# A fused encoder layer on one core: the steps of the state-space unit handed out one for each block of k's and q's projections, where k's blocks took two

## The chip, the cores and the metric

One Trainium2 chip, of which the kernel uses one core. The metric is the device time of the whole kernel in microseconds (us); the median of several runs is quoted. TensorE (PE) does the matmuls, VectorE (DVE) and GpSimd (POOL) elementwise work, ScalarE (ACT) activation functions and scaled copies; SyncE (SP) issues most DMAs.

## The reference

The layer takes `x` of 1024 tokens by 1024 columns in float32. The first half of it, in which the change lies, is `x <- x + W_out . groupRMS(concat[gMLP, S5, attention](W_in . RMSNorm(x)))`; a mixture of 16 experts follows. The three mixers share one input projection `W_in`. Cut to what matters here:

```python
def s5_mixer(u, ...):                      # u: 1024 tokens x 256 channels, 16 groups of 16 channels
    bu = einsum('gph,blgh->blgp', b_bar, ug)             # 64 complex states a group
    _, states = lax.associative_scan(combine, (a, bu), axis=1)
    y = einsum('ghp,blgp->blgh', c_mat, states).real
    y = gelu(y + d * u)
    return y * sigmoid(y @ glu_w + glu_b)

def band_attention(q, k, v, q_g, k_g, rel_bias):   # 8 heads of 64
    q, k = rms_norm(q, q_g), rms_norm(k, k_g)
    ...                                    # each chunk of 64 tokens sees itself and the 8 chunks before it
```

## The kernel before, in words

The normalised input stands transposed in SBUF as 8 pieces of 128 columns, each as a high and a low part (`hTh`, `hTl`), and every weight is split in the same way when it arrives: `load_w` fetches four pieces of 256 rows by 512 columns (`rw`), ACT copies the high part (`wh`, line 126) and DVE subtracts (`wl`, line 127). A product is then three matmuls (lines 130 to 132: high by high, low weight, low input).

A *block* is the projection of 128 tokens on 512 columns: 8 input pieces by 3 matmuls, 24 matmuls into one of two PSUM banks (`pj`, tag `acc`). The kernel does 8 blocks of k, then 8 of q, then 8 of v. For k and q each block is followed by a scaled copy (`kt` or `qt`, line 617), a square (`sqk`, line 619) and a sum over each head (`s`, line 620); every second block adds a reciprocal root on DVE (nine small instructions, lines 109 to 118: `rq_h`, `rq_y`, `rq_a`, `r`) and a product (line 624). v's blocks (`vt`, line 877) are interleaved with the transposition of k and q per head (`k_T`, `q_T`: lines 651 to 681) and with the first two sets of attention scores (lines 711 to 723), for which the Exp function's table is loaded on ACT at line 864.

The state-space unit S5 is a Python generator, `s5()`, that gives up control 21 times; `tick(n)` runs its next n steps. The steps in order:

- 1 to 3: transposed input (`u5`), powers and rotations for the first groups, `taps(0)`.
- 4 to 15: four rounds b = 0 to 3 of four groups each, three steps a round. The first step is `scan(b)` and `outputs(b)`: PE makes `s5v` (line 517, 16 matmuls), DVE multiplies by the rotation, adds, and scans (`zz`, lines 519, 520 and 522), POOL and DVE rotate back (`f`, line 527), and the output taps `w2` are made (lines 534 to 538; the trace calls the tile `w`). The second is `rotation(b+1)` (`cs`, `cst`: lines 504 and 505 on DVE, 506 to 509 on POOL). The third is `taps(b+1)` (`s5a` on PE, lines 483 and 484, whose copies are ACT's), `result(b)` (`s5y` on PE, lines 546 and 547; Gelu on ACT, line 549) and `powers(b+2)` (lines 473 to 475).
- 16 to 19: two halves of the gate: transpositions (`yTp` on PE, line 577; `yT` on ACT, line 579), then `glu` on PE (line 584), a sum on DVE (line 586), Sigmoid on ACT (line 587), a product on POOL (line 589).
- 20 and 21: a norm of each half of `y5`: square on ACT (line 598), sum on DVE (line 601), root, product on POOL.

After v's blocks `tick(100)` runs whatever steps are left, and attention follows. Tiles of the second PSUM tag, `big`, have three buffers, which S5's `s5a`, `s5v`, `s5y`, `yTp` and `glu` share with the transpositions of k and q and with the scores. Weights live in a ring of SBUF buffers; the pieces 0 and 1 of q's weights (written r0, r1 below; r2 and r3 are the others) are in a second ring.

In which order the instructions of these loops stand on an engine is made by the scheduler of the language from the program's order, free buffers and its own estimate of readiness; each engine then works strictly through its own queue. Attention's order is written out by hand and begins behind v's last block.

Of the kernel before, what the change touches and what calls it, by code (L numbers as in the profile page):

```python
# [31 lines left out]
def trunk(tc, A, dbg=None, upto="all"):  # L32
# [35 lines left out]
    def slot(name, shape, dt=F32, far=None):  # L68
        far = name in FAR if far is None else far
        return slots.tile(shape, dt, name=name, tag="far" if far else "slot", bufs=FARS if far else SLOTS)  # L70
# [7 lines left out]
    def acc(name, shape, dt=F32):  # L78
        return psum.tile(shape, dt, name=name, tag="acc", bufs=2)

    def bc(ap, shape):
        return ap.to_broadcast(shape)
# [7 lines left out]
    def tick(n=1):  # L90

        while n and side:
            try:
                next(side[0])
                n -= 1
            except StopIteration:
                side.pop(0)
# [23 lines left out]
    def rsqrt(*args):  # L121
        for _ in rsqrt_steps(*args):
            pass
# [58 lines left out]
    def proj(out, sel, w, ks=range(KD)):  # L182
        his, los = w
        for k in ks:
            mm3(out, hT[k][:, sel], lT[k][:, sel], his[k], los[k], k == ks[0], k == ks[-1])
# [108 lines left out]
    def tmp(shape, p=128):  # L294
        n = 1
        for q in shape[1:]:
            n *= q
        o = carve["o"]
        carve["o"] = o + n
        assert o + n <= 1024  # L300
        v = carve["t"][0:p, o:o + n]
        if len(shape) == 3:
            v = v.rearrange("p (a b) -> p a b", a=shape[1])
        if len(shape) == 4:
            v = v.rearrange("p (a b c) -> p a b c", a=shape[1], b=shape[2])
        return v
# [102 lines left out]
    kt = tmp([128, NG, 16])  # L409
# [198 lines left out]
    def qk_proj(name, w):  # L608
        out = []
        for tb in range(NT):  # L610
            a = acc("pj", [128, 512])
            proj(a, slice(tb * 128, (tb + 1) * 128), w)
            if tb % 2 == 0:
                out.append(slot(name, [128, 2, 512]))
                s16 = small.tile([128, 2, 8], F32, name="s16")
                r16 = small.tile([128, 2, 8], F32, name="r16")
            act.activation(out[-1][:, tb % 2], a, AF.Copy, scale=rs[:, tb:tb + 1])
            sq = work.tile([128, 512], F32, name="sqk", tag="w2")
            act.activation(sq, a, AF.Square, scale=rs[:, tb:tb + 1])
            dve.tensor_reduce(s16[:, tb % 2], sq.rearrange("p (h c) -> p h c", c=64), axis=AX.X, op=OP.add)  # L620
            if tb % 2 == 1:
                rsqrt(r16.rearrange("p a b -> p (a b)"), s16.rearrange("p a b -> p (a b)"), 16, 1.0 / 64)
                ov = out[-1].rearrange("p t (h c) -> p t h c", c=64)
                dve.tensor_tensor(ov, ov, bc(r16[:, :, :, None], [128, 2, 8, 64]), op=OP.mult)
            tick(2 if name == "kt" else 1)
        return out

    kt_ = qk_proj("kt", W["k"])
    W["q"] = load_w(768, 512, (0, 1))
    qt_ = qk_proj("qt", W["q"])  # L630
    W["v"] = load_w(1792, 512, (3,))
    gqk = const("gqk", [128, 2])
# [1021 lines left out]
```

## Time and profile before

| | us |
|---|---|
| median of 3 runs | 834.27 |
| lowest, highest run | 831.81, 837.59 |
| the profiled execution | 835.0 |
| its span in the trace | 833.1 |

The profiled execution is the one whose rows are read below, so a sum over rows is made against 835.0 us. The span is cut into busy time, waits and the granted clock of TensorE: a stretch's clock of 1.00 is 2.4 GHz, and 0.50 would be 1.2 GHz. "Waits" lists the idle time of an engine by what ended it. In the profiled execution k's blocks run from about 93.5 us to 171 us, q's from 183 us to 234 us and v's to 282.5 us; between k's and q's blocks lies a stretch of 12 us with S5's last round and half of its gate.

### The profile page before, as it was taken

The numbers are of one execution on the slowest core, as the hardware profiler recorded it, in microseconds if no ns is written. First come the engines' busy times: TensorE is split into PE (matmuls) and PEld (weight loads), VectorE is DVE, ScalarE is ACT, GpSimd is POOL, SyncE is SP. The second block draws the span as 40 slices with busy tenths as digits, with TensorE's granted clock in tenths as the row PEclk, the third lists the DMA queues.
The fourth block names the chain that finished last, engine by engine and source line by source line (L and its number), as shares of the span: only waits on it lengthen the run. The fifth ranks groups of instructions, "written<-read, shape, count | busy, mean of one in ns | idle before, by whom it ended". The sixth has DMA issues, their size and how long they took to land. (4 is left out here: it accounts for less than half of the span.)

```text
span 833.1 us, 13661 instructions
## 1 busy us (share of the span) xinstructions
PE 755.7 (91%) x5024; PEld 640.0 (77%) x5025; DVE 530.1 (64%) x1266; ACT 400.9 (48%) x751; POOL 200.4 (24%) x235
## 2 busy tenths in 40 slices
PE   5999998989999887888888999968899999999995
PEld 4878777868888777888887888747678778888884
DVE  5866799873651467787877544677675774575541
ACT  6763432223343467777774323434454654464441
POOL 0000245411410332212101121112242433243221
PEclk9999999999999989999999999998999999999998
DMA  8423011330000400001045323286889999899663
GB/s 312 138 57 102 6 15 15 54 114 0 2 1 1 126 26 2 1 27 52 2 132 188 140 101 127 76 306 201 286 283 279 328 349 315 223 308 309 130 154 54
DMA packets 56516, 111.31 MB, mean 134 GB/s; under 512 B 24272, under 2 KB 28880, under 8 KB 56432
## 3 DMA queue, kind: packets, MB, share of 16 engines
q1 hardware_dynamic: 46880, 84.14, 30.0%
q0 software_dynamic: 6480, 23.60, 11.9%
q10 hardware_dynamic: 3072, 2.49, 1.0%
q8 instruction: 47, 0.77, 0.4%
q14 instruction: 37, 0.30, 0.1%
HBM read 90.05 MB, written 20.17 MB: 132 GB/s over the span
## 5 line engine op out<-in xcount | busy, mean ns | idle before, releaser
L130 PE MATMUL pj<-wh,hTh 128*128 128x512 f32 x256 | 104.2, 408 | 0.4 <-ACT hTh L209 0.3
L131 PE MATMUL pj<-wl,hTh 128*128 128x512 f32 x256 | 101.6, 397 | 0.0
L132 PE MATMUL pj<-wh,hTl 128*128 128x512 f32 x256 | 100.5, 398 | 0.1
L130 PE MATMUL gup<-gh,hgh 128*128 128x256 f32 x304 | 89.8, 295 | 1.7 <-ACT hgh L1278 0.2
L132 PE MATMUL gup<-gh,hgl 128*128 128x256 f32 x304 | 86.8, 286 | 3.1 <-DVE hgl L1282 3.1
L131 PE MATMUL gup<-gl,hgh 128*128 128x256 f32 x304 | 86.0, 283 | 0.0
L1325 PE MATMUL yp<-rwd,hh 128*128 128x256 f32 (+1 forms) x264 | 84.4, 457 | 0.0
L977 DVE TENSOR_TENSOR gl<-rwg,gh 128x1024 fp32r<-128x1024 f32 x64 | 78.0, 1241 | 7.3 <-ACT gh L972 6.5
L972 ACT ACTIVATE gh<-rwg 128x1024 fp32r<-128x1024 f32 x64 | 64.1, 1052 | 1.4 <-ACTq L1581 0.4
L1325 PEld LDWEIGHTS yp<-rwd,hh 128*128 128x128 f32 x264 | 45.8, 190 | 23.2 <-issue 17.4
L130 PEld LDWEIGHTS gup<-gh,hgh 128*128 128x128 f32 x304 | 57.9, 191 | 6.1 <-ACT y L1334 5.2
L132 PEld LDWEIGHTS gup<-gh,hgl 128*128 128x128 f32 x304 | 58.2, 191 | 4.5 <-DVE hgl L1282 3.6
L131 PEld LDWEIGHTS gup<-gl,hgh 128*128 128x128 f32 x304 | 58.2, 191 | 0.1
L132 PEld LDWEIGHTS pj<-wh,hTl 128*128 128x128 f32 x256 | 48.1, 188 | 12.7 <-DVE hTl L210 1.3
L130 PEld LDWEIGHTS pj<-wh,hTh 128*128 128x128 f32 x256 | 48.5, 190 | 12.0 <-ACT hTh L209 1.3
L1337 POOL DMA_INDIRECT out<-y,ix x22 | 38.2, 1735 | 78.9 <-ACT y L1334 45.9
L127 DVE TENSOR_TENSOR ptl<-ps,pth 128x640 fp32r<-128x640 f32 (+2 forms) x53 | 39.7, 749 | 26.5 <-ACT pth L126 26.1
L131 PEld LDWEIGHTS pj<-wl,hTh 128*128 128x128 f32 x256 | 48.4, 189 | 10.4
L130 PE MATMUL po<-pth,v_h 128*64 128x128 f32 x236 | 47.8, 232 | 2.9 <-DVE oc L765 2.0
L1334 ACT ACTIVATE y<-yp 128x512 f32<-128x512 f32 (+1 forms) x44 | 21.6, 491 | 59.6 <-PE yp L1325 59.6
L1262 POOL DMA_INDIRECT hg<-h2d,ix x22 | 23.8, 1080 | 105.2 <-PE yp L1325 69.5
L732 PE MATMUL ps<-ident,st 128*128 128x128 f32 x240 | 38.5, 290 | 9.8 <-ACT st L723 9.2
(390 smaller groups left out, 1974.9 us busy)
## 6 DMA issues: line engine op xcount, KB each, us to landing
rwg<-in_w_gu SPq DMA_DIRECT2D x62, 512.0 KB, 9.0
rwd<-in_w_down SPq DMA_DIRECT2D x32, 512.0 KB, 6.6
rw<-in_w_in SPq DMA_DIRECT2D x18, 512.0 KB, 5.1
xt<-in_x SPq DMA_DIRECT2D x8, 512.0 KB, 9.2
rwo<-in_w_out SPq DMA_DIRECT2D x8, 512.0 KB, 4.6
xr<-in_x SPq DMA_DIRECT2D x8, 512.0 KB, 4.3
out<-x SPq DMA_DIRECT2D x8, 512.0 KB, 2.6
h2d<-h SPq DMA_DIRECT2D x8, 512.0 KB, 2.9
```

Source lines behind the costliest of these rows:

```text
L127: (eng_lo or dve).tensor_tensor(lo, src, f32(hi), op=OP.subtract)
L130: pe.matmul(out, ah, bh, start=first, stop=False)
L131: pe.matmul(out, ah, bl, start=False, stop=False)
L132: pe.matmul(out, al, bh, start=False, stop=last)
L732: pe.transpose(pp[:, b], st[:, b * 128:(b + 1) * 128], ident)
L972: act.activation(pc[1], pc[0], AF.Copy)
L977: eng.tensor_tensor(t, pc[0], f32(pc[1]), op=OP.subtract)
L1262: pool.indirect_dma_start(out=self.hg, out_offset=None, in_=h2d[:, :], in_offset=bass.IndirectOffsetOnAxis(ap=self.ix, axis=0))
L1325: pe.matmul(self.py[nb][0], self.hh[r], self.ex.d[r][:, ns], start=(r == 0), stop=(r == 1))
L1334: act.activation(self.y[:, ns], p, AF.Copy)
L1337: pool.indirect_dma_start(out=out[:, :], out_offset=bass.IndirectOffsetOnAxis(ap=self.ix, axis=0), in_=self.y, in_offset=None, compute_op= ...
```

## The change

One line of `qk_proj`, which both k and q pass through:

```diff
@@ -622,7 +622,7 @@
                 ov = out[-1].rearrange("p t (h c) -> p t h c", c=64)
                 dve.tensor_tensor(ov, ov, bc(r16[:, :, :, None], [128, 2, 8, 64]), op=OP.mult)
-            tick(2 if name == "kt" else 1)
+            tick(1)
         return out
```

Before, k's 8 blocks hand out steps 1 to 16, and q's first five blocks steps 17 to 21. Now k's blocks hand out steps 1 to 8, q's blocks 9 to 16, and v's first five blocks 17 to 21. So S5's rounds b = 2 and 3 move from k's blocks to q's, and the gate and the norms from q's to v's. Up to attention the order on the engines is made anew; from there on it is the same on all of them.

DVE's queue where k ends and q begins. `wl` are the low parts of q's weight pieces, `sqk` and `s16` belong to k's last block, `w2` and `f5` to the S5 round that stands there. Before, that is the round b = 3:

```order
L537 COPY w2_1563<-w2_1563 64x512
L527 TENSOR_TENSOR f5_1559<-cs_1468,zz_1552 128x4x127
L538 TENSOR_SCALAR w2_1563<-w2_1563 64x512
L127 TENSOR_TENSOR wl_1656<-rw_1653,wh_1655 128x1024
L127 TENSOR_TENSOR wl_1662<-rw_1659,wh_1661 128x1024
L620 TENSOR_REDUCE s16_1537<-sqk_1595 128x8
L109 TENSOR_SCALAR rq_h_1598<-s16_1537 128x16
```

Now it is the round b = 1, with the rotation for b = 2 behind it:

```order
L527 TENSOR_TENSOR f5_1417<-cs_1278,zz_1410 128x4x127
L538 TENSOR_SCALAR w2_1421<-w2_1421 64x512
L504 TENSOR_TENSOR cs_1471<-scr_667 128x512
L505 TENSOR_TENSOR cst_1472<-scr_667 128x512
L127 TENSOR_TENSOR wl_1494<-rw_1491,wh_1493 128x1024
L620 TENSOR_REDUCE s16_1395<-sqk_1453 128x8
L127 TENSOR_TENSOR wl_1482<-rw_1479,wh_1481 128x1024
L109 TENSOR_SCALAR rq_h_1456<-s16_1395 128x16
L127 TENSOR_TENSOR wl_1500<-rw_1497,wh_1499 128x1024
L111 TENSOR_SCALAR rq_y_1458<-rq_h_1456 128x16
L127 TENSOR_TENSOR wl_1488<-rw_1485,wh_1487 128x1024
```

`wl_1482` is r0, the piece that q's first block needs first, `wl_1488` is r1, `wl_1494` r2 and `wl_1500` r3. All four splits now stand in one piece with the end of k; before, r0 and r1 stood further back, behind the product of line 624.

PE's queue at the same place. Before, the high-by-high matmul of q's first block (`pj_1665`) stood behind the gate's matmuls:

```order
L584 MATMUL glu_1697<-gluw_1628,yT_1639 128x256 x3
L130 MATMUL pj_1665<-wh_1643,hTh0_84 128x512
L584 MATMUL glu_1697<-gluw_1628,yT_1639 128x256 x2
L131 MATMUL pj_1665<-wl_1644,hTh0_84 128x512
L132 MATMUL pj_1665<-wh_1643,hTl0_92 128x512
```

Now q's first two blocks (`pj_1503`, `pj_1574`) begin with one such matmul each, beside the result of round b = 1, and then need `wl_1482`:

```order
L546 MATMUL s5y_1556<-w2_1421,f5_1417 128x128 x2
L130 MATMUL pj_1503<-wh_1481,hTh0_84 128x512
L547 MATMUL s5y_1556<-tp5_1346,u5_0_1009 128x128
L546 MATMUL s5y_1556<-w2_1421,f5_1417 128x128 x2
L547 MATMUL s5y_1556<-tp5_1346,u5_0_1009 128x128
L130 MATMUL pj_1574<-wh_1481,hTh0_84 128x512
L131 MATMUL pj_1503<-wl_1482,hTh0_84 128x512
L132 MATMUL pj_1503<-wh_1481,hTl0_92 128x512
```

The gate's and the transpositions' instructions left these places. The gate now stands among v's blocks, on ACT between the two Exp's of lines 864 and 723:

```order
L877 ACTIVATE vt_2035<-pj_2010,rs_100 128x512
L864 ACT_TABLE_LOAD
L864 ACTIVATE one_2009<-vt_2035 128x1
L677 ACTIVATE kh_2056<-pk_2051 64x2x128 x2
L677 ACTIVATE kh_2057<-pk_2051 64x2x128 x2
L587 ACT_TABLE_LOAD
L587 ACTIVATE sg5_2046<-sg5_2046 128x1024
L877 ACTIVATE vt_2035<-pj_2071,rs_100 128x512
```

Here `vt_2035` of `pj_2010` and of `pj_2071` are v's first and second block. Before, no S5 instruction stood among v's.

## Rows read from the trace of the kernel before

**Rows 1.** Busy time by stage: the stretch in us and its length, then busy us (and instructions) of PE, PE's weight loads, DVE, ACT and POOL, then TensorE's granted clock, the DMA engines' share and GB/s. The stages are k's blocks, the passage from k to q, q's blocks and v's blocks.

```profile
93.50:171.00 77.50, 71.55 (x415) 61.32 (x413) 67.71 (x127) 24.19 (x54) 36.63 (x35) 0.98 0.19 23
171.00:183.00 12.00, 8.47 (x45) 7.01 (x44) 10.66 (x20) 4.78 (x6) 1.61 (x2) 0.86 0.43 119
183.00:234.00 51.00, 51.00 (x226) 41.45 (x225) 23.21 (x72) 18.98 (x24) 11.84 (x10) 1.00 0.05 19
234.00:282.50 48.50, 48.50 (x231) 39.60 (x230) 15.39 (x46) 17.89 (x43) 6.22 (x16) 1.00 0.06 16
```

**Rows 2.** What PE waited for from 93.5 us to 283 us: who waits, for whom, the sum in us, how often, the longest.

```profile
PE s5y L546 <- DVE w L538: 5.8, 4, 3.7
PE s5y L546 <- POOL f L527: 2.0, 2, 1.3
PE glu L584 <- ACT yT L579: 1.1, 1, 1.1
PE yTp L577 <- ACT y L549: 0.6, 1, 0.6
```

**Rows 3.** The matmuls on PE's timeline at which four of these waits ended: start, us, instruction, and in brackets the idle time ahead of it and what ended it. They are the results of the rounds b = 1, 2 and 3, and the gate.

```profile
141.37 0.38 PE L546 MATMUL s5y<-w,f 128*128 128x128 f32 x1 [3.71 <-DVE w L538]
155.31 0.38 PE L546 MATMUL s5y<-w,f 128*128 128x128 f32 x1 [0.84 <-DVE w L538]
172.36 0.38 PE L546 MATMUL s5y<-w,f 128*128 128x128 f32 x1 [1.34 <-POOL f L527]
178.85 0.48 PE L584 MATMUL glu<-gluw,yT 128*128 128x256 f32 x1 [1.11 <-ACT yT L579]
```

**Rows 4.** Two stretches with a lower granted clock, columns as in Rows 1.

```profile
137.00:146.00 9.00, 5.29 (x32) 5.10 (x32) 8.80 (x13) 2.00 (x7) 5.71 (x7) 0.81 0.00 0
177.50:184.00 6.50, 5.39 (x19) 4.17 (x17) 4.43 (x9) 2.92 (x3) 0.30 (x1) 0.74 0.68 202
```

**Rows 5.** PE's timeline around the round b = 2, between two blocks of k: the block that follows `s5v`, the start of `s5a` and of `s5y`, and the next block.

```profile
147.26 0.48 PE L130 MATMUL pj<-wh,hTh 128*128 128x512 f32 x1
152.94 0.29 PE L483 MATMUL s5a<-bcm,w1t 128*128 128x16 f32 x2
154.09 0.39 PE L546 MATMUL s5y<-w,f 128*128 128x128 f32 x2
157.79 0.48 PE L130 MATMUL pj<-wh,hTh 128*128 128x512 f32 x1
```

**Rows 6.** DVE's timeline, the round b = 1 with a reciprocal root among its instructions: the first, the copy of line 537 and the last of the chain.

```profile
130.84 1.21 DVE L519 TENSOR_TENSOR zz<-s5v,cs 128x1024 f32<-128x1024 f32 x1
135.81 1.54 DVE L537 COPY w<-w 64x512 f32<-64x512 f32 x1
140.08 1.23 DVE L538 TENSOR_SCALAR w<-w 64x512 f32<-64x512 f32 x1
```

**Rows 7.** DVE's timeline, the round b = 2 without one, and what stands behind it.

```profile
147.61 1.23 DVE L519 TENSOR_TENSOR zz<-s5v,cs 128x1024 f32<-128x1024 f32 x1 [0.25 <-PE s5v L517]
154.07 1.19 DVE L538 TENSOR_SCALAR w<-w 64x512 f32<-64x512 f32 x1
155.29 1.65 DVE L504 TENSOR_TENSOR cs<-scr 128x512 f32<-128x512 f32 x1
156.86 0.68 DVE L505 TENSOR_TENSOR cst<-scr 128x512 f32<-128x512 f32 x1
157.46 0.67 DVE L620 TENSOR_REDUCE s<-sqk 128x8 f32<-128x512 f32 x1
```

**Rows 8.** DVE's timeline at the end of k: the round b = 3's last instruction and two weight splits.

```profile
172.87 0.42 DVE L538 TENSOR_SCALAR w<-w 64x512 f32<-64x512 f32 x1
173.32 2.36 DVE L127 TENSOR_TENSOR wl<-rw,wh 128x1024 fp32r<-128x1024 f32 x2
```

**Rows 9.** POOL's timeline: two instructions that ran while DVE had those of Rows 6 and 7 in hand.

```profile
135.80 1.27 POOL L527 TENSOR_TENSOR f<-cs,zz 128x508 f32<-128x508 f32 x1 [5.44 <-DVE rq_y L118]
155.05 1.34 POOL L509 TENSOR_TENSOR cs<-cs,cst 128x512 f32<-128x512 f32 x1
```

**Rows 10.** ACT's timeline: two successive copies of q's blocks, without S5 between them on PE; and the two table loads of the stretch from 93.5 us to 283 us, the second with the head copies ahead of it.

```profile
216.60 0.69 ACT L617 ACTIVATE qt<-pj,rs 128x512 f32<-128x512 f32 x1 [3.07 <-PE pj L132]
222.20 0.69 ACT L617 ACTIVATE qt<-pj,rs 128x512 f32<-128x512 f32 x1 [4.33 <-PE pj L132]
189.87 1.28 ACT L587 ACT_TABLE_LOAD   x1
239.98 1.19 ACT L677 ACTIVATE kh<-pk 64x256 fp32r<-64x256 f32 x3
241.19 1.28 ACT L864 ACT_TABLE_LOAD   x1
```

**Rows 11.** Groups of instructions by line and shape, of DVE from 93.5 us to 283 us and of ACT from 183 us to 234 us: busy us, mean ns of one, then idle time ahead of them and what ended it. They are the gate's and the norms'.

```profile
L586 DVE TENSOR_TENSOR sg<-glu,row 128x1024 f32<-128x1024 f32 x2 | 2.4, 1220 | 1.5 <-PE glu L584 1.5
L587 ACT ACTIVATE sg<-sg 128x1024 f32<-128x1024 f32 x2 | 2.1, 1058 | 4.0 <-DVE sg L586 4.0
L601 DVE TENSOR_REDUCE s5s<-sq 128x16 f32<-128x1024 f32 x2 | 2.4, 1219 | 3.6 <-ACT sq L598 3.6
```

## The prediction

> **What bounds the kernel now.** I read the busy time by stage first [rows 1]. The reader is to see that PE is the bound wherever q's and v's blocks run: 51.00 of 51.00 us and 48.50 of 48.50 us, at a clock of 1.00, while DVE has 23.21 and 15.39 us of work there and ACT 18.98 and 17.89. In k's stage it is different: DVE is busy for 67.71 of 77.50 us and PE for 71.55. Between k and q, DVE has 10.66 of 12.00 us and PE only 8.47. So S5's DVE work is packed into the stretch where DVE is already nearly full. The stages with half of DVE free get little of it.
>
> The waits of PE come next [rows 2]: 5.8 us of the product `s5y` for DVE's last tap instruction, 2.0 us for POOL's `f`, 1.1 us of the gate for `yT`, 0.6 us of `yTp` for the Gelu. That is 9.5 us in eight waits, four of which [rows 3] show the pattern: 3.71 us at the round b = 1, 0.84 at b = 2, 1.34 at b = 3, 1.11 at the gate. All are S5's: its PE part comes back to the queue before its DVE part is done.
>
> Then the clock [rows 4]. It falls in two stretches, each around such waits: 0.81 over 9.00 us about the wait of 3.71, and 0.74 over 6.50 us after the four waits between k and q. At two levels, 2.4 and 1.2 GHz, these means say 2 x 0.19 x 9.00 = 3.4 us and 2 x 0.26 x 6.50 = 3.4 us at the lower one, and half of each is lost: 1.7 + 1.7 = 3.4 us. All that could be won is so 9.5 + 3.4 = 12.9 us.
>
> **The change part by part.** No instruction of the work itself is removed; the rounds and the gate move. So the sum is: which of these 12.9 us stay away, and what comes new.
>
> *Rounds b = 0, 2 and 3.* Between a round's `s5v` and its `s5y` there stood one block of 24 matmuls; now there are two. A block takes 222.20 - 216.60 = 5.60 us [rows 10], and the taps `s5a` take 154.09 - 152.94 = 1.15 us [rows 5], so PE has 2 x 5.60 + 1.15 = 12.35 us to do, 11.2 for b = 3, which has no taps. DVE's chain takes 154.07 + 1.19 - 147.61 = 7.65 us without a root among it [rows 7] and 140.08 + 1.23 - 130.84 = 10.5 us with one [rows 6], from 0.35 us after `s5v` (147.61 against 147.26, [rows 5, 7]). 10.9 us fit into 12.35 and barely into 11.2. So these waits go. I leave 0.5 us for them; the bounds are 0 and the rival below.
>
> *Round b = 1.* It now stands across the end of k, with one block of 24 between `s5v` and its taps, and no root ahead of its last instruction. That is the b = 2 of before, with its wait of 0.84 us [rows 3]; I take 1.0 us (bounds 0.8, and 1.8 with b = 3's two waits).
>
> *The passage to q.* This is the new cost. Let 0 be the end of k's last block on PE. By the b = 2 of before, `w2` is finished at 155.26 - 152.94 = 2.3 us, say 2.4 [rows 5, 7]. Behind it DVE now has, in this order, the rotation (1.65 and 0.68 us with their overlap, to 4.6: 157.46 is 2.2 us behind 155.26, [rows 7]), the split of r2 (half of 2.36, so 1.2: 5.8, [rows 8]), the sum of `sqk` (0.6: 6.4), and only then the split of r0: to 7.6 us if each runs alone. The rotation and the powers of the next round are on POOL at that time. Two such neighbours were seen to stretch a DVE instruction: the copy of line 537 took 1.54 us beside POOL's `f`, and the rotation 1.65 where its companion took 0.68 [rows 6, 7, 9]. With one such stretch the split ends at 8.7. I take 8.3.
>
> The Trainium skill (SBUF — State Buffer, "Who interferes with whom") says a DVE instruction with two SBUF inputs contends with a GpSimd instruction that reads SBUF, and the one that comes second is blocked for the other's whole length. The 1.54 and 1.65 us agree. Alone by that rule, with POOL's 1.34 us in full, r0 would come at 8.9; without it at 7.6.
>
> PE meanwhile waits to 2.4, needs 157.79 - 155.31 = 2.5 us for `s5y` [rows 3, 5] and 0.5 us for the two high-by-high matmuls of q (24 in 5.60 us make one 0.233), and is out of work at 5.4. It idles to 8.3: 2.9 us, taken as 3.0 (bounds 2.2 and 3.4, and 4.0 if r1's split is late too). Behind that stand 11 matmuls, 2.6 us, while DVE splits r3 and r1 (2.4 us and two small ones): covered within 0.1 us. A wait of this size drew 1.7 us of low clock both times before [rows 4]; I add it (bounds 0 and 3.4).
>
> *The gate and the norms* leave the passage (their waits of 1.1 and 0.6 us are within the 9.5) and stand among v's blocks, where DVE is idle for 33 us and ACT for 31 [rows 1]. They bring there two sums of 1.22 us, two Sigmoids of 1.06 and two reductions of 1.22 [rows 11], and ACT gets one more table load, since Sigmoid stands between the two Exp's: 1.28 us [rows 10]. PE's own gate matmuls are only moved. I take 0; the bound above is the rival below, and nothing can be won there, since PE has no gap.
>
> The Trainium skill (ScalarE: Activation LUTs, "What ACT_TABLE_LOAD costs") speaks against this order: a switch of sets costs about 2.66 us with the drain, and functions of one set should stand together. The trace shows 1.28 us for the load. By the page the estimate is 2.66 us on ACT, and the sum stays the same as long as ACT has that to spare.
>
> *Sum*: 12.9 - (0.5 + 1.0 + 3.0 + 1.7) = 6.7 us. 835.0 - 6.7 = 828.3 us in the terms of the profiled execution; the median of the runs, 834.27, lies 0.7 below it, so 827.6 us.
>
> **The rivals.**
>
> *A, the forecast*: 827.6 us, with an own range of 823.5 to 831.5 by the bounds above.
>
> *B, the passage is covered.* If the split of r0 runs before the rotation's POOL part gets in its way, and 2.2 us or less of idling do not lower the clock, only about 1.5 us come new: 12.9 - 1.5 = 11.4, so 823.6 and, against the median, 822.9 us. For it speaks that the 0.84 us wait drew no visible low stretch [rows 3, 4]; against it that four splits stand behind one another on one engine.
>
> *C, the waits come back in q.* If the roots of q's blocks stand among the chains as in b = 1 (10.5 us where 7.65 would do, [rows 6, 7]) and POOL's part starts late, two of the rounds wait as before, each 3.71 us and 1.7 of clock: 6.7 - 2 x 5.4 = -4.1; with one round 6.7 - 5.4 = 1.3. I take one as the likely form: 833.7, against the median 833.0 us. For it speaks the narrow 0.3 us at b = 3; against it DVE's 28 idle us in q's stage.
>
> *D, the slower side: v's blocks wait for ACT's queue.* The copy of v's second block now stands behind the first block's copy, a table load, four `kh` copies, a second load and the Sigmoid, which itself waits for `glu` and DVE's sum. Until it is done, its PSUM bank is not free, and v's fourth block cannot start. By rows, that is 5.6 us for the block, some 2 for the transpositions and the gate on PE, 0.7 + 1.28 + 0.2, four times 0.4, 1.28 and 1.06 [rows 10, 11]: some 13 us after the end of q. The fourth block would start at three blocks of 48.50 / 8 = 6.1 us and the gate's PE work of some 5: at about 23 us. It decides from there: if the Sigmoid ends later than 23 us after q, PE waits. The price, if three blocks meet such a wait as large as the largest before, is 3 x (3.71 + 1.7) = 16.2 us: 835.0 - 6.7 + 16.2 = 844.5, against the median 843.8 us. Against it stand those 10 us of slack.
>
> That the change does nothing is excluded: the order shows the rounds at their new places.
>
> **How the numbers follow.** Chances: A 0.52, B 0.20, C 0.19, D 0.09. The forecast is A's 827.6. The range goes from 821.5, a little under B, to 834.5, over C; D and the outer ends of B and C are left out. One per cent of 834.27 is 8.3 us, about what a measurement of this kernel can tell from no change. Faster by over that means below 825.9: nearly all of B (0.18) and the lower third of A (0.16), so 0.34. Slower by over that means above 842.6: most of D and the far end of C, 0.08. The rest is 0.58.
>
> **What would show it.** In the trace after: PE's waits of `s5y` for DVE shrink from 5.8 us to about 1.0, all of it at the round that stands across k's end; the stretch at 0.81 about the 3.71 us wait is gone; a new wait of about 3 us of q's line 131 for `wl` appears right behind that round, with half-clock matmuls after it; `yTp` and `glu` wait for nothing among v's blocks, and PE stays full from there to attention. Wrong would be: a wait of an `s5y` above 2 us among q's blocks (C), no wait of line 131 (B), or idle time of v's `pj` for ACT (D). If the waits go as I say and the time does not, the gain was lost in attention, whose order is the same.

## The result, and the profile after

The changed kernel takes 826.38 us (median of 5 runs, 823.16 to 829.04) against 834.49 us of the kernel before beside it: a ratio of 0.9889, 95% interval 0.9846 to 0.9931. That is 8.1 us less, where 6.7 were forecast. Measured again on another occasion it took 825.63 us, a ratio of 0.9889 again (0.9857 to 0.9921). The profiled execution is the fastest of the first five: 823.16 us, span 821.4.

First the stages, columns as in [rows 1], for k's blocks, the passage, q's blocks and v's:

```profile
93.50:151.35 57.85, 57.85 (x315) 49.03 (x314) 46.15 (x98) 19.73 (x45) 19.63 (x18) 1.00 0.11 12
151.35:161.00 9.65, 6.33 (x44) 5.47 (x44) 9.59 (x9) 5.95 (x10) 7.37 (x5) 0.98 0.24 65
161.00:215.50 54.50, 54.50 (x279) 45.76 (x279) 39.52 (x86) 13.51 (x23) 15.35 (x18) 0.97 0.26 53
215.50:273.40 57.90, 57.82 (x280) 47.74 (x278) 25.24 (x73) 28.23 (x52) 14.92 (x21) 1.00 0.04 11
```

k's stage went from 77.50 us with PE at 71.55 to 57.85 us with PE at 57.85. q's and v's stages grew by the S5 work that came to them, and PE is still busy all through them; DVE's load in q rose from 23.21 to 39.52 us and cost PE nothing there. Only the passage is left with idle PE, and DVE is busy for 9.59 of its 9.65 us. The waits say the same. What PE waited for from 93.5 us to 274 us, against [rows 2]:

```profile
PE pj L131 <- DVE wl L127: 2.4, 1, 2.4
PE s5y L546 <- DVE w L538: 0.9, 1, 0.9
```

Eight waits have become two, and 9.5 us have become 3.3. Both stand where k ends, next to each other on PE's timeline, and behind them the clock falls as in [rows 4]:

```profile
153.54 0.38 PE L546 MATMUL s5y<-w,f 128*128 128x128 f32 x1 [0.87 <-DVE w L538]
159.16 0.50 PE L131 MATMUL pj<-wl,hTh 128*128 128x512 f32 x1 [2.45 <-DVE wl L127]
```

```profile
155.00:160.00 5.00, 2.55 (x18) 2.08 (x17) 5.00 (x7) 2.30 (x6) 4.15 (x2) 1.00 0.34 104
160.00:164.00 4.00, 4.00 (x12) 3.14 (x11) 3.98 (x10) 0.00 (x0) 0.03 (x1) 0.57 0.79 216
```

A clock of 0.57 over 4.00 us is 2 x 0.43 x 4.00 = 3.4 us at 1.2 GHz, half of it lost: 1.7 us, the same as each of the two stretches before.

What held r0 up is on DVE's timeline, with POOL's beside it. The block of k ended at 151.15 us:

```profile
152.32 1.17 DVE L538 TENSOR_SCALAR w<-w 64x512 f32<-64x512 f32 x1
153.52 1.65 DVE L504 TENSOR_TENSOR cs<-scr 128x512 f32<-128x512 f32 x1
155.09 0.68 DVE L505 TENSOR_TENSOR cst<-scr 128x512 f32<-128x512 f32 x1
155.69 1.21 DVE L127 TENSOR_TENSOR wl<-rw,wh 128x1024 fp32r<-128x1024 f32 x1
156.83 0.67 DVE L620 TENSOR_REDUCE s<-sqk 128x8 f32<-128x512 f32 x1
157.42 1.69 DVE L127 TENSOR_TENSOR wl<-rw,wh 128x1024 fp32r<-128x1024 f32 x1
159.03 1.03 DVE L109 TENSOR_SCALAR rq_h<-s 128x16 f32<-128x16 f32 x1
```

```profile
155.85 2.18 POOL L508 TENSOR_TENSOR cs<-cs,cst 128x512 f32<-128x512 f32 x1 [1.23 <-DVE cst L505]
157.99 2.04 POOL L474 TENSOR_TENSOR w1t<-ak,bcm 128x512 f32<-128x512 f32 x1
```

`w2` is finished 2.34 us after the block (2.4 in the prediction), r2's split 5.75 us after it (5.8), and r0's 7.96 us (7.6 if undisturbed, 8.3 taken). r2's split began 0.16 us ahead of POOL's instruction at 155.85 and took 1.21 us; r0's began while that instruction still ran, to 158.03, and took 1.69.

**Where the time came from.** To compare kernels without what attention does, take the stretch from ACT's copy of k's first block (the expectations below call it k's second copy) to its copy of v's last: 282.63 - 102.59 = 180.04 us before and 273.64 - 102.74 = 170.90 us after, so 9.14 us. Of these, the waits make 9.5 - 3.3 = 6.2 and one of two half-clock stretches 1.7. The rest, 1.3 us, is busy time of PE: 170.56 us stand in the stretch before and 167.50 after, 3.1 us less, of which 1.7 is the clock. It goes with the waits too. From start to start, a wait costs PE more than the idle time listed for it: the last matmul ahead of it shows some 0.16 us of busy time that the next one would have covered (`s5y`'s take 0.28 us and otherwise start 0.11 us apart), and the first one behind it holds up the next by another 0.10 us. Six waits fewer make some 1.6 us, an estimate, against the 1.3 measured. The spans differ by 833.1 - 821.4 = 11.7 us; the other 2.6 us are mostly attention's, and not the change's (below).

### The profile page after: what moved, and what is told of

The parts are those of the page before. It is cut to its first block, busy times and chain, and to the rows that moved or that the text cites. A ratio compares the mean times of both kernels' runs of the same rounds, so it can differ in the third digit from the quotient of the medians.

```text
span 821.4 us, 13661 instructions
## 1 busy us (share of the span) xinstructions
PE 749.3 (91%) x5024; PEld 635.3 (77%) x5025; DVE 533.7 (65%) x1266; ACT 401.9 (49%) x752; POOL 202.9 (25%) x235
## 5 line engine op out<-in xcount | busy, mean ns | idle before, releaser
L1325 PE MATMUL yp<-rwd,hh 128*128 128x256 f32 (+1 forms) x264 | 86.1, 465 | 0.0
L130 PEld LDWEIGHTS pj<-wh,hTh 128*128 128x128 f32 x256 | 48.6, 190 | 12.9 <-ACT hTh L209 2.4
L126 ACT ACTIVATE pth<-ps 128x640 fp32r<-128x640 f32 (+2 forms) x53 | 34.3, 646 | 25.3 <-PE ps L732 24.6
```

What stands on the lines that cost most here:

```text
L126: act.activation(hi, src, AF.Copy)
L130: pe.matmul(out, ah, bh, start=first, stop=False)
L1325: pe.matmul(self.py[nb][0], self.hh[r], self.ex.d[r][:, ns], start=(r == 0), stop=(r == 1))
```

## The experiments

All ratios are against the kernel before, on the same chip; its median was 834.49 us beside the changed kernel and 834.70 to 835.98 us beside the others. The changed kernels have 4 to 12 runs each. The table gathers the profiled execution's stretch of the paragraph above, PE's waits up to the end of v, and the median.

| kernel | steps in k, q | stretch, us | waits, us | median, us | ratio (95%) |
|---|---|---|---|---|---|
| before | 16, 5 | 180.04 | 9.5 | 834.49 | |
| changed | 8, 8 | 170.90 | 3.3 | 826.38 | 0.9889 (0.9846-0.9931) |
| half | 12, 8 | 175.94 | 6.4 | 829.95 | 0.9935 (0.9909-0.9961) |
| k1q2 | 8, 13 | 179.69 | 9.7 | 835.02 | 0.9996 (0.9973-1.002) |
| k9 | 9, 8 | 171.20 | 4.2 | 825.69 | 0.9889 (0.9857-0.9922) |
| k7 | 7, 8 | 171.44 | 3.9 | 826.27 | 0.9881 (0.9851-0.9912) |
| k9_far3 | 9, 8 | 168.09 | 2.4 | 824.94 | 0.9873 (0.9836-0.9909) |
| k9_far3_p3 | 9, 8 | 171.92 | 4.6 | 827.35 | 0.9903 (0.9872-0.9934) |
| after_far23 | 8, 8 | 169.96 | 2.6 | 824.03 | 0.9857 (0.9819-0.9894) |
| nosig | 8, 8 | 170.94 | 3.4 | 825.66 | 0.9883 (0.9854-0.9912) |

**Is it the cover, or the idle DVE?** The theory is that a round waits when one block of matmuls must cover its chain on DVE, and not when two do. The rival is that q's stage, with half of DVE idle, would have taken the rounds at any pace. `k1q2`:

```diff
-            tick(1)
+            tick(1 if name == "kt" else 2)
```

> k's blocks hand out one step as in the changed kernel, q's blocks two: the rounds b = 2 and 3 and the gate all fall into q, the norms too, and nothing of S5 into v. Theory (cover by matmuls decides, not how idle DVE is): the passage as in the changed kernel (0.9 and 2.4 us); in q, with DVE half idle, s5y still waits 1 to 2 us for each of b = 2 and 3, and the gate 0.5 to 1.7 us; so 3 to 6 us above the changed kernel, 829 to 832 us. Rival (what helped is that DVE is idle in q's stage, so one block is cover enough there): no wait in q over 0.5 us, and 826 us; if the gate among v's blocks costs something in the changed kernel, below 826.

PE's waits of this kernel from 93.5 us to the end of v:

```profile
PE pj L131 <- DVE wl L127: 3.6, 3, 2.5
PE s5y L546 <- DVE w L536: 2.8, 1, 2.8
PE s5y L546 <- DVE w L538: 2.4, 3, 1.1
PE s5y L546 <- POOL f L527: 0.9, 1, 0.9
```

In q's stage `s5y` waits 2.77 and 1.05 us at the round b = 2 and 0.88 and 0.51 at b = 3, and the clock is 0.70 from 180 to 190 us. The whole gain is gone: 835.02 us. The direction is the theory's and the size larger than it said (829 to 832). At b = 3 DVE's chain took 7.28 us, without a root, and one block did not cover it. At b = 2 the chain took 11.46 us, with a rotation's instruction and a sum in it and POOL's instructions beside it, so that this wait is not the cover's alone; and line 131 waits 1.2 us more than in the changed kernel. The gate, for which 0.5 to 1.7 us were expected, waits for nothing. Idle DVE time does not help a chain that is too long for its cover.

`half` keeps the old pace for k's first four blocks:

```diff
-            tick(1)
+            tick(2 if name == "kt" and tb < 4 else 1)
```

> Half of the change: k's first four blocks hand out two steps each as before, the other four one. The round b = 2 ends with k, b = 3 and the gate fall into q, one norm into v. Theory (a round waits when one block of 24 matmuls must cover its chain, and does not when two do): the rounds b = 0 and 1 stay as before and wait, 0.9 to 1.4 us and 2.5 to 4 us, the second with its stretch of half clock; b = 2, b = 3 and the gate wait for nothing or under 1 us in all; the passage holds no round and line 131 waits under 1.5 us. PE idle from 93.5 us to the end of v 4 to 6 us against 9.5 before and 3.3 changed: 826 to 829 us. Rival (the gain comes from k's later rounds and the emptied passage alone): no wait at b = 0 and 1, 821 to 823 us.

```profile
120.59 0.49 PE L546 MATMUL s5y<-w,f 128*128 128x128 f32 x2 [0.62 <-POOL f L527]
122.34 0.49 PE L546 MATMUL s5y<-w,f 128*128 128x128 f32 x2 [0.79 <-DVE w L538]
140.79 0.80 PE L546 MATMUL s5y<-w,f 128*128 128x128 f32 x2 [3.71 <-DVE w L538]
```

In the kernel before, the round b = 0 waited like this:

```profile
121.17 0.49 PE L546 MATMUL s5y<-w,f 128*128 128x128 f32 x2 [0.63 <-POOL f L527]
122.91 0.49 PE L546 MATMUL s5y<-w,f 128*128 128x128 f32 x2 [0.78 <-DVE w L538]
```

The rounds b = 0 and 1 wait as before (1.4 us, and 3.71 as in [rows 3]), the later ones not at all, and line 131 waits 1.1 us. About half of the gain is left: 829.95 us, a little over the 826 to 829 expected. So each round's wait goes with its own cover, and they add up.

Two blocks are enough only as long as the chain is shorter than they are. In the changed kernel the round b = 2 has a root among its chain. Its first and last DVE instruction, and the `s5y` that needs it:

```profile
173.65 1.22 DVE L519 TENSOR_TENSOR zz<-s5v,cs 128x1024 f32<-128x1024 f32 x1
183.73 0.42 DVE L538 TENSOR_SCALAR w<-w 64x512 f32<-64x512 f32 x1
185.68 0.61 PE L546 MATMUL s5y<-w,f 128*128 128x128 f32 x4
```

The chain takes 10.5 us and ends 1.5 us before PE comes for it. In `k9`, a kernel of the next group, the root stands in the round b = 3, which has no taps, and DVE waits 4.08 us in it for POOL's part of `w2`:

```profile
189.48 1.21 DVE L519 TENSOR_TENSOR zz<-s5v,cs 128x1024 f32<-128x1024 f32 x1
200.93 0.42 DVE L538 TENSOR_SCALAR w<-w 64x512 f32<-64x512 f32 x1
201.41 0.49 PE L546 MATMUL s5y<-w,f 128*128 128x128 f32 x2 [0.66 <-DVE w L538]
```

Here the chain takes 11.87 us, and PE waits 0.66 us in spite of two blocks.

**Does the gate cost anything among v's blocks?** `nosig` puts Exp in the place of Sigmoid, another function, so that ACT changes no tables there:

```diff
-            act.activation(sg, sg, AF.Sigmoid)
+            act.activation(sg, sg, AF.Exp)
```

> The changed kernel with Exp in the place of the gate's Sigmoid: a different function, and no change of tables among v's blocks; two table loads (the Sigmoid's and the one back to Exp) fall away on ACT. Theory (ACT has 10 us to spare among v's blocks): no wait of PE goes, the time is that of the changed kernel within 1 us, 825 to 828 us, and the stretch from k's second copy to the end of v stays 170.9 us. Rival (the switch costs the time of the load and more, 1.3 us and over for each): 2.6 us and more below, 822 to 824 us, the stretch 168 us.

The stretch is 170.94 us against 170.90, the median 825.66. The two loads cost no time outside ACT. On ACT's timeline of the changed kernel they stand like this:

```profile
216.17 0.67 ACT L617 ACTIVATE qt<-pj,rs 128x512 f32<-128x512 f32 x1
226.14 1.59 ACT L677 ACTIVATE kh<-pk 64x256 fp32r<-64x256 f32 x4 [1.69 <-PE pk L668]
227.75 1.28 ACT L587 ACT_TABLE_LOAD   x1
229.05 1.06 ACT L587 ACTIVATE sg<-sg 128x1024 f32<-128x1024 f32 x1
231.74 0.69 ACT L877 ACTIVATE vt<-pj,rs 128x512 f32<-128x512 f32 x1 [1.63 <-PE pj L132]
248.85 1.28 ACT L723 ACT_TABLE_LOAD   x1
```

The Sigmoid ends at 230.1 us, some 14 us behind q's last block (the rival D says 13; its terms add up to 13.7), and ACT then still waits 1.63 us for PE's second block. The load at 227.75 starts with the copies' end and the Sigmoid 0.02 us after the load's: the switch cost 1.28 us and nothing more on this timeline. The Trainium skill (ScalarE: Activation LUTs, "What ACT_TABLE_LOAD costs") adds a drain and comes to about 2.66 us; this trace shows no such gap. Its rule to keep functions of one set together (section "Table sets: the hidden batching unit") was worth nothing here, where ACT had the time to spare.

**What holds the passage up?** Here my theory was that the rotation and `w2` ahead of r0's split are the whole cost. `k9` moves the round out of the passage, `k7` the rotation alone:

```diff
-            tick(1)
+            tick(2 if name == "kt" and tb == 0 else 1)     # k9
+            tick(0 if name == "kt" and tb == 7 else 1)     # k7
```

> k's first block hands out steps 1 and 2, every other block one: k's blocks do steps 1 to 9, so the round b = 1 ends with k's last block and no round lies across the passage to q. Theory (what is left of waits in the changed kernel is DVE's queue at the passage: w2's last instruction, the rotation and then r0's split): the wait of s5y for w2 (0.87 us) is gone, line 131's wait for r0 (2.45 us) falls to between 0 and 1.5 us, the half-clock stretch behind it (1.7 us lost) goes or shrinks: 3 to 5 us below the changed kernel's 826.4, so 821 to 823 us. Rival (the passage costs its 2 to 3 us whatever S5 does there, because four splits follow one another on DVE): line 131 still waits 2 us or more and the time is that of the changed kernel, 826 us.

> k's last block hands out no step: the rotation of the round b = 2 no longer stands on DVE between the round b = 1 and the splits of q's weights; w2 still does, and the first of the s5y matmuls still stands ahead of q's block on PE. Theory: s5y waits about 0.9 us as in the changed kernel; r0's split ends 2.2 us earlier, but only 1 matmul of s5y and not all 12 are there to cover it: line 131 waits about 1.1 us instead of 2.45. 1 to 3 us below the changed kernel: 823 to 825 us. Rival (POOL's instructions, not the rotation on DVE, hold the split up): line 131 waits over 2 us, 826 us.

Both missed. In `k9` the wait of `s5y` in the passage is gone, but line 131 waits 3.51 us, longer than in the changed kernel (the other 0.66 us of the table is the round b = 3 shown above). DVE's timeline there, from r2's and r3's splits to r0's:

```profile
152.35 3.44 DVE L127 TENSOR_TENSOR wl<-rw,wh 128x1024 fp32r<-128x1024 f32 x2
155.71 0.67 DVE L620 TENSOR_REDUCE s<-sqk 128x8 f32<-128x512 f32 x1
156.31 0.47 DVE L490 TENSOR_TENSOR s5d<-s5d 16x64 f32<-16x64 f32 x1
156.78 0.67 DVE L473 TENSOR_TENSOR w1t<-ak,bcm 128x512 f32<-128x512 f32 x1
157.56 0.69 DVE L475 TENSOR_TENSOR w1t<-w1t 128x512 f32<-128x512 f32 x1
158.25 1.22 DVE L127 TENSOR_TENSOR wl<-rw,wh 128x1024 fp32r<-128x1024 f32 x1
```

With the rotation gone, the taps' correction and the powers of the round stand in its place, and the two splits beside POOL take 3.44 us together. In `k7` r0 and r1 are the first splits, but POOL's rotation runs beside them and they take 3.96 us together; line 131 waits 3.9 us in three waits. Both rivals came out: line 131 waits over 2 us and the medians, 825.69 and 826.27 us, are those of the changed kernel. DVE has four splits and a sum to do, and in all of these kernels some S5 work of DVE's or POOL's stands beside them. Which part of it costs how much is not shown.

The next three change which pieces come first. The pieces named in the argument go into the ring whose buffers come free late:

```diff
-    W["q"] = load_w(768, 512, (0, 1))
+    W["q"] = load_w(768, 512, (2, 3))     # after_far23, on the changed kernel
+    W["q"] = load_w(768, 512, (3,))       # k9_far3, on k9
```

> The changed kernel with r0 and r1 in the early ring and r2 and r3 in the late one, so that r0 is the first split behind the rotation and r1 the second. But with r0 thought ready early, half of s5y's matmuls now stand behind q's first block on PE. Theory: s5y waits 0.9 us; r0's split ends 2.2 us earlier, but 1.2 us less of cover stands ahead of it; then r1, r2 (each behind a sum or a root's instruction) come late by 0.5 to 1 us each: line 131 waits 2 to 3.5 us in all, so nothing is won: 825 to 828 us. Rival (only r0's place in DVE's queue counts): line 131 waits under 1 us, 822 to 823 us.

> The same without moving the powers: r0, r1 and r2 are split first, then the sum, the tap correction and the powers of the last groups, then r3. Theory: line 131 waits 0.5 to 1 us for r1 or r2 and 1 to 2 us for r3, 1.5 to 2.5 us in all against 3.5 in k9; 822 to 825 us. Rival (the order of the pieces does not matter): 3 us or more, 825 to 826 us.

`after_far23` has its 2.04 us wait of line 131 as expected and 0.64 of `s5y`; r1 to r3 came in time, and half of `s5y` ran between them. Its time, 824.03 us, is below the 825 to 828 expected. `k9_far3` waits 0.33 and 2.03 us, 2.4 in all, within the 1.5 to 2.5 expected, and in this run nothing of the clock was lost behind it. The last one also moves the powers of the last groups two steps on, out of the passage:

```diff
             if b < 3:
                 rotation(b + 1)
+                if b == 2:
+                    powers(3)
 ...
-            if b < 2:
+            if b < 1:
                 powers(b + 2)
```

> k9 (k hands out steps 1 to 9) with two things taken off DVE's queue at the passage: q's first three weight pieces instead of its last two go into the ring whose buffers come free early, so that r0, r1 and r2 are split first and r3 last; and the powers for the last groups are made two steps later, out of the passage. Theory (line 131's 3.5 us in k9 are r0's place behind two other splits, a sum, the tap correction and the powers, which themselves wait for POOL): r0's split ends when PE is done with s5y; line 131 waits at most 1.5 us in all, no stretch of half clock, no wait of s5y; 3 to 6 us below k9 and the changed kernel: 820 to 823 us. Rival (the passage costs its 3 us in any order, since DVE's and POOL's work beside each other is what is late): line 131 waits 2.5 us or more in all, and 825 to 826 us.

It missed: r0 to r2 came in time, but r3's split had been put behind eight small instructions of the root, at 161.23 us, and line 131 waited 2.48 us; and the powers, now in q, came late for their taps, 2.14 us. How DVE and POOL got in each other's way differs too. DVE's three splits and POOL's rotation in `k9_far3_p3`:

```profile
153.49 3.49 DVE L127 TENSOR_TENSOR wl<-rw,wh 128x1024 fp32r<-128x1024 f32 x3
```

```profile
153.65 4.48 POOL L508 TENSOR_TENSOR cs<-cs,cst 128x512 f32<-128x512 f32 x1 [3.71 <-DVE cst L505]
```

and the same in `k9_far3`, the splits one by one:

```profile
153.38 1.22 DVE L127 TENSOR_TENSOR wl<-rw,wh 128x1024 fp32r<-128x1024 f32 x1
154.51 2.31 DVE L127 TENSOR_TENSOR wl<-rw,wh 128x1024 fp32r<-128x1024 f32 x1
156.74 2.08 DVE L127 TENSOR_TENSOR wl<-rw,wh 128x1024 fp32r<-128x1024 f32 x1
```

```profile
153.54 2.19 POOL L508 TENSOR_TENSOR cs<-cs,cst 128x512 f32<-128x512 f32 x1 [3.71 <-DVE cst L505]
155.70 2.04 POOL L474 TENSOR_TENSOR w1t<-ak,bcm 128x512 f32<-128x512 f32 x1
```

In the one, DVE's three splits run at 1.16 us each and POOL's instruction ends 1.15 us after the last of them; in the other they take turns. Each split that finds a POOL instruction running ends 1.1 us after that instruction, and each POOL instruction ends 0.9 to 1.1 us after the split that it found running. The moved powers are not the reason: in its second profile (below) `k9_far3` itself shows the first picture:

```profile
153.52 3.49 DVE L127 TENSOR_TENSOR wl<-rw,wh 128x1024 fp32r<-128x1024 f32 x3
```

```profile
153.69 4.48 POOL L508 TENSOR_TENSOR cs<-cs,cst 128x512 f32<-128x512 f32 x1 [3.71 <-DVE cst L505]
```

The Trainium skill (SBUF — State Buffer, "Who interferes with whom") says that the order of issue decides who blocks. The trace agrees for the first split, which began 0.16 us ahead of POOL's instruction each time and kept its 1.2 us. Why the second split goes ahead of the waiting POOL instruction in one execution and behind it in another is not settled.

**Is one of these better than the change?** Three kernels on one chip:

> The changed kernel once more, on one chip with the next two. Theory: 825 to 828 us; its stretch from k's second copy to v's last one 170.9 us as before, whatever attention's clock does.

> The changed kernel with r0 and r1 in the early ring, once more. By its first profile line 131 waits 2.0 us instead of 2.4 and s5y 0.6 instead of 0.9, and the stretch is 169.9 us, 1 us shorter than the changed kernel's. Theory: 1 to 2 us below it. Rival (the first 824.0 us came from attention's clock): within 0.5 us of it.

> Nine steps in k and three pieces in the early ring, once more. By its first profile no wait of s5y, 2.4 us of line 131, no stretch of half clock up to attention, and a stretch of 168.1 us, 2.8 us shorter than the changed kernel's. Theory: 2 to 4 us below the changed kernel, and below the other variant by 1 to 2 us. Rival: within 1 us of it.

The changed kernel took 825.63 us (0.9889, 0.9857 to 0.9921), `after_far23` 823.82 (0.9864, 0.9830 to 0.9898), `k9_far3` 825.60 (0.9876, 0.9845 to 0.9907). `after_far23` is 1.8 us below the changed kernel, with 0.94 us less in the stretch both times (169.96 and 169.97 against 170.90 and 170.91), but the intervals overlap: likely better, not shown. For `k9_far3` the rival was right, and its stretch shows why: 168.09 us in the first profile and 274.21 - 103.23 = 170.98 in the second. The second time line 131 waited 2.68 us and the clock fell behind it.

**Attention's clock.** Attention's instructions stand in the same order in all these kernels, yet its time differs from run to run of one kernel. In the two profiles of the changed kernel, from v's last copy to the router's first matmul, it is 171.9 and 174.8 us, and in those of `k9_far3` 177.0 and 172.6 us. Two stretches of 20 us of the changed kernel, in the first profile and then in the second:

```profile
273.60:293.60 20.00, 14.47 (x121) 13.26 (x119) 12.73 (x35) 15.04 (x36) 10.34 (x24) 0.83 0.41 125
293.60:313.60 20.00, 14.63 (x158) 13.59 (x159) 15.24 (x40) 14.03 (x33) 5.63 (x7) 1.00 0.01 2
```

```profile
273.30:293.30 20.00, 15.63 (x120) 13.93 (x118) 12.75 (x35) 14.92 (x36) 10.21 (x23) 0.74 0.40 124
293.30:313.30 20.00, 14.66 (x144) 13.62 (x145) 14.88 (x38) 13.51 (x32) 5.61 (x7) 0.92 0.01 2
```

The clock's mean is lower by 0.09 and 0.08 in these, and by 0.04 in each of two more from 353 to 393 us: 5.0 us of PE's time at full speed. The end of attention came 2.9 us later; PE is not busy throughout there, with 14.5 to 15.6 of these 20 us. The kernel before has 174.9 us in its profile. So the 11.7 us between the two spans are 9.1 of the change and some 3 of attention's clock.

## Why the prediction was right

**The bound and the removable part.** Right: all eight waits and both half-clock stretches were S5's, and no other wait came in k's, q's or v's blocks but the one named. The 12.9 us count a wait by its idle time alone; the 0.26 us that each cost on top were left out.

**Rounds b = 0, 2 and 3.** 0.5 us were left for them; there is no wait at all. The cover argument is shown by `half` and `k1q2`: with one block back, each round waits again. At b = 2, with a root, 12.35 - 10.9 = 1.45 us of room were forecast and 1.5 measured. The narrow 0.3 us at b = 3 were not put to the test here: the root fell to b = 2, and the chain of b = 3 took 7.0 us. That was luck; in `k9` the root fell to b = 3, as the rival C has it, and cost 0.66 us and not the 3.71 that C took for a round.

**Round b = 1.** 1.0 us forecast, 0.87 measured.

**The passage.** 3.0 us forecast, 2.45 measured; r0's split came at 7.96 us where 8.3 was taken. The order of DVE's queue gave this, and the times of before its size. Of the two durations from which a stretch of 1.1 us was taken, the 1.54 us are a copy's, which has one input, so that only the 1.65 bear on the rule as quoted; r0's split lost 0.5 us, since only 0.6 us of POOL's instruction were left when it began. That the rotation and `w2` are what stands in the way is only half of it: without the round (`k9`) or DVE's part of the rotation (`k7`) there, the wait was 3.5 and 3.9 us.

**Clock.** One stretch of 1.7 us forecast, one measured. Its size is not certain at such a wait: the two profiles of `k9_far3`, with waits of 2.4 and 2.7 us, lost nothing and 3.4 us.

**The gate.** No cost forecast, none found: `nosig` has the same stretch to 0.04 us, and the Sigmoid's place in ACT's queue left the room that D's working said, though its terms add up to 13.7 us and not 13.

**The sum.** 6.7 us forecast in the profile's terms; 9.1 measured in the stretch that the change touches. Of the 2.4 us between, 0.7 (1.00 - 0.87 + 3.00 - 2.45) are the two waits at the passage, 0.5 the rounds that didn't wait, and the rest, some 1.3, the busy time of PE that no term had. The medians' 8.1 us lie between, with attention's run-to-run clock in them; that 827.6 us came within 1.2 us of the median is in part luck. A's own range is a little wider than its bounds, which give 824.4 and not 823.5 at the low end. Of the rivals, B's total (11.4) was as far off in the stretch as A's, and its mechanism did not happen; C and D did not happen.

## What to carry to other kernels

Side work that comes back to the bound engine needs cover by that engine's own work between its two visits, one chain long; how idle its other engines are does not replace it. When a stage is left, look at what the side engine still has in its queue ahead of the first thing that the next stage needs, for it is where the waits gather; putting the pieces there in the order of need was worth about 2 us at most here (`after_far23`), and that is not shown. Judge such changes by the stretch that they touch as well as by the whole time, where another stage varies by 3 us from run to run.

## What the runs showed of the hardware

- Waits of nearly the same size draw a half-clock stretch in one run and not in another: `k9_far3` waited 0.33 and 2.03 us and kept a clock of 1.00, and 2.68 us in its second profile with a clock of 0.70 and 0.61 in the two stretches of 5 us from 160 us on; `after_far23` waited 2.04 us and had a clock of 0.73 from 155 to 160 us.
- A wait of PE cost some 0.26 us beyond the idle time listed for it: 0.16 us of the last matmul ahead of it, 0.10 us at the first one behind it.
- Attention's time varied by 2.9 us between two profiles of the changed kernel and by 4.5 us between two of `k9_far3`, at the same order of instructions.
- A split of 128x1024 took 1.21 us alone, and the same beside a POOL product of 128x512 that began after it; one that began while such a product ran took 1.69 to 2.3 us. The POOL products that began while a split ran took 2.0 to 2.2 us, where 1.34 was seen in [rows 9]; in two profiles DVE's splits kept their pace and POOL's instruction took 4.48 us.
- A change of ACT's function table cost 1.28 us and left no further gap.
